# Holding 96 weight-sum transfers to their step with a small ScalarE copy, and laying them in three stages

## The chip, the cores and the metric

The kernel runs on one core of one Trainium2 chip. The metric is the device time of one execution in microseconds. The core has five engines that run their own instruction streams in order: PE (TensorE, matrix products), DVE (VectorE), ACT (ScalarE), POOL (GpSimd) and SP (SyncE, here only an issuer of transfers). Transfers run on 16 DMA engines; SP issues most of them, POOL those that this change is about.

## The reference, cut to what matters

The program is a two-layer decoder trunk over 1024 tokens of width 1024, in float32: a short gated convolution layer with a SwiGLU feed-forward block, then a latent-attention layer with a second SwiGLU block.

```python
def short_conv_mixer(h, w_in, conv_w, w_out):
    u = h @ w_in
    gate_b, gate_c, val = jnp.split(u, 3, axis=-1)
    z = gate_c * val
    conv = sum(conv_w[k] * zp[:, k:k + s] for k in range(CONV_WIDTH))   # zp: z, padded
    return (gate_b * conv) @ w_out

def swiglu_ffn(h, w13, w2):
    g, u = jnp.split(h @ w13, 2, axis=-1)
    return (jax.nn.silu(g) * u) @ w2

h = h + short_conv_mixer(rms_norm(h, conv_norm_g), conv_w_in, conv_w, conv_w_out)
h = h + swiglu_ffn(rms_norm(h, conv_ffn_norm_g), conv_ffn_w13, conv_ffn_w2)
k_nope, k_pe, v = shared_mla_kv(h, ...)
h = h + mla_mixer(rms_norm(h, mla_norm_g), ..., k_nope, k_pe, v, ...)
h = h + swiglu_ffn(rms_norm(h, mla_ffn_norm_g), mla_ffn_w13, mla_ffn_w2)
return rms_norm(h, final_norm_g)
```

## The kernel before

Every float32 product is made of three matmuls (`three`, lines 152 to 155) on a high and a low part of each operand. ACT makes the high part with a cast (line 112), and DVE or POOL subtracts it to get the low part (line 113). The large projections use a seven-product scheme for 2 x 2 blocks, which needs sums of blocks of the operands.

**Stages.** The program runs through: the conv input projection (class `Quad`, 12 quads of 7 products, tile `q`), the conv output projection (class `Plain`, tile `pl`), the up projection of the first feed-forward block (22 quads of 7 products, tile `q` again), its down projection (class `Down`, tile `dn`), the latents, the attention, and then `Plain`, up and `Down` once more for the second block. One product of a quad is 12 matmuls of 128x512.

**What sets the order.** Outside the attention the order is written by hand. `Steps` (lines 255 to 278) holds a list of PE work, one entry per product, and for each entry the functions to emit ahead of it (`before`) and behind it (`after`); all are emitted in that order, each to its own engine's stream. A step number is so a place in every stream, but nothing makes an engine wait for the step: an engine runs its stream as far ahead as its own waits let it. The attention is ordered by a planner; its order on PE, DVE and SP is the same in both kernels.

**The transfers that are changed.** `Down` needs, for four of its seven products, sums of blocks of the weight `w2`; these four sums (`mw_f` in DRAM, 6 groups each) are built for each feed-forward block with no compute engine at all, by transfers from DRAM to DRAM that POOL issues: a plain copy, or a copy that adds into its destination (`weight_sums`, lines 872 to 893; the issues are lines 889 and 887). Eight rounds over six groups make 48 transfers of 512 KB (256 KB for the last group) for each block, 96 in all. Line 887 waits for the transfers that it adds onto. `Down` loads the results on SP (line 613).

Before the change, lines 898 and 899 emit the first 48 at steps 4, 6, 8, ... of the conv input projection, and lines 908 and 909 the other 48 at steps 6, 9, 12, ... of the first up projection. POOL has in these stages one other task: in the conv input projection it forms two sums of weight columns for each quad (lines 377 and 380, two instructions of 128x512 for 12 quads).

**What stands around them.** SP's stream holds at the end of the conv input projection, in this order: loads of the stored conv result (`m<-md_conv`, line 548) and of the output weight (`wp`, line 503), eight loads of the residual stream (`h<-hd`, line 478, 512 KB each), the last two stores of the conv result (line 719), and the load of the last group of that result, which must wait for these stores. ACT splits that group (`mh<-m`, line 112) before PE can go on with `pl`. The up projections load a 512 KB tile of weights twice per quad (`wr`, line 361) into five buffers.

Of the kernel before, what the change touches and what calls it, by code (L numbers as in the profile page):

```python
# [9 lines left out]
F32 = mybir.dt.float32  # L10
# [6 lines left out]
P = 128  # L17
# [32 lines left out]
def trunk(ctx, tc, aps, out):  # L50
    nc = tc.nc
    A = aps
# [19 lines left out]
    small = ctx.enter_context(tc.tile_pool(name="small", bufs=2))  # L72
# [21 lines left out]
    def work(name, shape=None, dt=F32):  # L94
        return pslot(name, "t", 9, dt, shape or [P, S])
# [63 lines left out]
    ones = const.tile([P, P], F32, name="ones")  # L159
# [8 lines left out]
    for nm in ("conv_norm_g", "conv_w", "conv_ffn_norm_g", "kv_norm_g", "mla_norm_g", "kv_latent_norm_g",  # L168
               "mla_q_norm_g", "mla_ffn_norm_g", "final_norm_g"):
        a = A[nm]  # L170
        if len(a.shape) == 3:
            a = a.rearrange("a b c -> (a b c)")
        elif len(a.shape) == 2:
            a = a.rearrange("a b -> (a b)")
        n = a.shape[0] // P
# [71 lines left out]
    st = Stream()  # L247
    hd = dram.tile([KD, P, S], F32, name="hd")
    md = {"conv": dram.tile([KD, P, S], F32, name="md_conv")}
# [5 lines left out]
    class Steps:  # L255
# [13 lines left out]
        def run(self):  # L269
            end = max([len(self.pe)] + [n + 1 for n in (*self.pre, *self.post)])  # L270
            with tc.manual_schedule():
                for n in range(end):
                    for fn in self.pre.get(n, ()):
                        fn()
                    if n < len(self.pe):
                        self.pe[n]()
                    for fn in self.post.get(n, ()):
                        fn()
# [166 lines left out]
    def up(steps, quads, op):  # L445

        head, n0 = quads[:FILL], len(steps.pe)
        a, b = quads[:2]
        n = {}

        for x, i in [(a, 1), (b, 1), (a, 2), (b, 2), *((x, i) for x in head[2:] for i in (1, 2)),
                     *((x, i) for i in (5, 6, 7, 4, 3) for x in (a, b)),
                     *((x, i) for x in quads[2:] for i in ((5, 6, 7, 4, 3) if x in head else (1, 2, 5, 6, 7, 4, 3)))]:
            n[x, i] = x.add(steps, op, i)
        for x in head:
            steps.before(n[x, 1] - 9, x.load_a)
            steps.before(n[x, 1] - 2, x.pair)
        for x in quads:
            n5 = n[x, 5]
            if x in head:  # L460
                steps.before(n5 - 9, x.load_a, x.load_b)
            else:
                steps.before(n5 - 11, x.load_a)
                steps.before(n5 - 10, x.load_b)
                steps.before(n5 - 5, x.pair)
            e = 0 if x.eng is nc.vector else 1
            steps.before(n5 - 3 - e, x.sum3, x.sum1)
            steps.before(n5 - 2, lambda x=x: x.half(5))
            steps.before(n[x, 6] - 2, x.sum2, lambda x=x: x.half(6))
            steps.before(n[x, 7] - 2, lambda x=x: x.half(7))  # L470
            steps.before(n[x, 4] - 2, lambda x=x: x.half(4))
            steps.before(n[x, 3] - 2, x.sum4, lambda x=x: x.half(3))
        return n0
# [250 lines left out]
    steps = Steps()  # L724
# [99 lines left out]
    def ffn_quads(w13, m):  # L824
        wv = w13.rearrange("a k n -> (a k) n").rearrange("(k p) n -> p k n", p=P)

        first = {}

        def store(i, j, t):
            nc.sync.dma_start(m[i - 1, j], t)  # L830

        def one(j):

            last, j0, box = j >= KF // 2, j % (KF // 2), {}

            def product(c1, c2):
                nc.vector.tensor_tensor(c1, c1, c2, ALU.mult)
                store(2 if last else 1, j0, c1[:, :512])
                if last:
                    store(3, j0, c1[:, 512:])  # L840
                    box["b"] = [(c[:, :512], c[:, 512:]) for c in (first.pop(j0), c1)]
                else:
                    first[j] = c1

            def left(c1, c2):
                (b11, b12), (b21, b22) = box["b"]
                box["s"] = work("msum")
                box["t1"], box["t2"] = box["s"][:, :512], box["s"][:, 512:]
                sub(5, box["t1"], b12, b11)

            def right(c1, c2):
                (b11, b12), (b21, b22) = box["b"]
                sub(6, box["t2"], b22, box["t1"])

            def low(c1, c2):
                (b11, b12), (b21, b22) = box["b"]
                sub(7, b12, b22, b12)

            def corner(c1, c2):
                (b11, b12), (b21, b22) = box["b"]  # L860
                sub(4, b21, box["t2"], b21)

            def sub(i, o, x, y):
                nc.vector.tensor_tensor(o, x, y, ALU.subtract)
                store(i, j0, o)

            done = [product, left, right, low, corner] if last else [product]
            return Quad(wv, j * P, DFF + j * P, AF.Silu, done, nc.vector)

        return [one(j + f) for j in range(KF // 2) for f in (0, KF // 2)]  # L870

    def weight_sums(w, out):


        wv, half = w.rearrange("(k p) n -> p k n", p=P), KF // 2
        groups = [list(range(k, min(k + 2, half))) for k in range(0, half, 2)]

        def one(i, src, add, g):
            o = [out[j, g][:, :len(groups[g]) * 512].rearrange("p (k m) -> p k m", m=512) for j in range(4)]
            if isinstance(src, tuple):  # L880
                (a, b), k = src, groups[g][0]
                k += b * half
                src = wv[:, k:k + len(groups[g]), (1 - a) * 512:(2 - a) * 512]
            else:
                src = o[src]
            if add:
                nc.gpsimd.dma_start(o[i], src, accum_op=ALU.add)
            else:
                nc.gpsimd.dma_start(o[i], src)

        stages = ((0, (1, 0), False), (3, (0, 0), False), (0, (1, 1), True), (3, (1, 0), True),
                  (1, 0, False), (1, (0, 0), True), (2, 1, False), (2, (0, 1), True))
        return [[lambda st=st, g=g: one(*st, g) for g in range(len(groups))] for st in stages]

    flat = lambda w: w.rearrange("a k n -> (a k) n")
    kp = lambda w: w.rearrange("(k p) n -> p k n", p=P)
    pairs = lambda a, b: [list(range(k, min(k + 2, b))) for k in range(a, b, 2)]
    for j, fn in enumerate(x for stage in weight_sums(flat(A["conv_ffn_w2"]), md["f1w"]) for x in stage):
        steps.before(4 + 2 * j, fn)
    bd = Boundary("conv_ffn_norm_g")  # L900
    n0 = len(steps.pe)
    steps.before(n0, lambda: load_h(range(KD)))
# [2 lines left out]
    bd.first(steps, e[1] + 5, (e[1] + 7, e[1] + 9, e[1] + 11, e[1] + 13))  # L905
    bd.second(steps, e[3] + 1)
    n0 = up(steps, ffn_quads(A["conv_ffn_w13"], md["f1"]), bd.op)
    for j, fn in enumerate(x for stage in weight_sums(flat(A["mla_ffn_w2"]), md["f2w"]) for x in stage):
        steps.before(n0 + 6 + 3 * j, fn)


    rd = dram.tile([2, P, S], F32, name="rd")
# [133 lines left out]
    n0 = len(steps.pe)  # L1046
# [285 lines left out]
    steps = Steps()  # L1332
    bd = Boundary("mla_ffn_norm_g")
# [1 line left out]
    e = pl.ends  # L1335
    bd.first(steps, e[1] + 4, (e[1] + 5, e[1] + 6, e[1] + 6, e[1] + 7))
    bd.second(steps, e[3] + 1)
    up(steps, ffn_quads(A["mla_ffn_w13"], md["f2"]), bd.op)


    fnorm = Norm()
# [73 lines left out]
```

## Time and profile before

| what | value |
|---|---|
| median of 3 runs | 2308.64 us (2300.48 to 2309.67) |
| profiled execution, own time | 2309.89 us |
| its span, first to last instruction | 2308.1 us |
| mean granted clock of PE | 0.96 |
| conv input projection, first to last product | 28.1 to 291.5 us |
| conv output projection | 291.5 to 431 us |
| first up projection | 431 to 885 us |
| second up projection | 1604 to 2058 us |

The profile is one execution, with times counted from the start of its span. Rows of a group give busy time and mean duration, and the idle time of the engine just before with what ended it. A row of a list in order of time gives start, duration, engine, line, operation and tiles; a bracket gives the idle time before it and the releaser. A duration of a matmul overlaps the next one, so the pace of PE is read from start to start. "SPq" rows are transfers as SP issues them.

### The profile page before, as it was taken

Reading aid. Unit: us, or ns where it says so; the run is one execution under the profiler, and the core shown is the slowest. Engines: PE = TensorE matmul, PEld = TensorE weight load, DVE = VectorE, ACT = ScalarE, POOL = GpSimd, SP = SyncE. Lnnn points to the kernel's source line nnn. Section 1 sums busy time; section 2 is a strip of 40 time slices with the busy share of each in tenths; the row PEclk is TensorE's granted clock in tenths of the full one; section 3 lists DMA queues with packets and bytes.
Section 4 is the critical chain, followed back from the end, with each engine's and each line's share of the span. In section 5 each row is a group of like instructions: output and inputs, shape, how many; then the busy total and the mean of one; then the engine's idle time right before and its main releaser. Section 6 shows DMA issues by size and latency. Waiting matters only on the chain. (4 is left out here: it accounts for less than half of the span.)

```text
span 2308.1 us, 26314 instructions
## 1 busy us (share of the span) xinstructions
PE 2152.8 (93%) x9869; PEld 1770.5 (77%) x9869; DVE 1525.6 (66%) x2291; ACT 833.6 (36%) x1321; POOL 249.7 (11%) x286
## 2 busy tenths in 40 slices
PE   7889939889999999999987999998899999999997
PEld 5677827767888888788866888887777888888786
DVE  4787714587777776877335777636787777777554
ACT  6322313342333333345223555424433333333443
POOL 0232422100000000000114333210000000000000
PEclk9999978899999999999888999998899999999998
DMA  8366799914332328565212223423334233376542
GB/s 269 113 145 178 185 317 283 262 37 146 114 114 92 114 97 324 194 210 169 62 32 61 64 70 77 168 82 113 97 101 137 94 112 99 107 263 221 177 169 77
DMA packets 271341, 331.67 MB, mean 144 GB/s; under 512 B 17745, under 2 KB 178718, under 8 KB 270894
## 3 DMA queue, kind: packets, MB, share of 16 engines
q1 hardware_dynamic: 244144, 265.86, 35.1%
q0 software_dynamic: 26784, 64.04, 11.3%
q8 instruction: 77, 1.26, 0.2%
q14 instruction: 50, 0.41, 0.1%
q10 hardware_dynamic: 286, 0.11, 0.0%
HBM read 251.83 MB, written 119.01 MB: 161 GB/s over the span
## 5 line engine op out<-in xcount | busy, mean ns | idle before, releaser
L153 PE MATMUL q<-xh,w_hi 128*128 128x512 f32 x1568 | 623.6, 398 | 28.7 <-ACT w_hi L112 27.3
L155 PE MATMUL q<-xh,w_lo 128*128 128x512 f32 x1568 | 623.2, 397 | 11.2 <-DVE w_lo L113 11.0
L154 PE MATMUL q<-xl,w_hi 128*128 128x512 f32 x1568 | 619.2, 395 | 5.1 <-DVE xl L303 5.0
L113 DVE TENSOR_TENSOR w_lo<-wr,w_hi 128x1024 fp32r<-128x1024 f32 (+1 forms) x336 | 263.2, 783 | 212.9 <-ACT w_hi L112 212.7
L153 PEld LDWEIGHTS q<-xh,w_hi 128*128 128x128 f32 x1568 | 299.6, 191 | 100.6 <-ACT w_hi L112 38.8
L155 PEld LDWEIGHTS q<-xh,w_lo 128*128 128x128 f32 x1568 | 299.2, 191 | 91.1 <-DVE w_lo L113 28.8
L112 ACT CAST w_hi<-wr 128x1024 fp32r<-128x1024 f32 (+1 forms) x336 | 225.3, 686 | 353.9 <-DVE wr L386 197.9
L154 PEld LDWEIGHTS q<-xl,w_hi 128*128 128x128 f32 x1568 | 299.2, 191 | 68.9 <-DVE xl L303 6.7
L155 PE MATMUL dn<-mp_hi,wp_lo 128*128 128x512 f32 x616 | 242.2, 393 | 4.9 <-DVE wp_lo L113 3.2
L153 PE MATMUL dn<-mp_hi,wp_hi 128*128 128x512 f32 x616 | 242.1, 393 | 0.5 <-ACT wp_hi L112 0.5
L154 PE MATMUL dn<-mp_lo,wp_hi 128*128 128x512 f32 x616 | 240.7, 391 | 0.4 <-DVE mp_lo L113 0.4
L113 DVE TENSOR_TENSOR mp_lo<-m,mp_hi 128x1024 fp32r<-128x1024 f32 x84 | 95.3, 1135 | 128.5 <-ACT mp_hi L112 128.5
L112 ACT CAST mp_hi<-m 128x1024 fp32r<-128x1024 f32 x84 | 82.2, 979 | 215.0 <-PE dn L154 206.6
L155 PEld LDWEIGHTS dn<-mp_hi,wp_lo 128*128 128x128 f32 x616 | 115.9, 188 | 35.9 <-DVE wp_lo L113 12.0
L154 PEld LDWEIGHTS dn<-mp_lo,wp_hi 128*128 128x128 f32 x616 | 116.0, 188 | 25.1 <-DVE mp_lo L113 0.8
L153 PEld LDWEIGHTS dn<-mp_hi,wp_hi 128*128 128x128 f32 x616 | 116.0, 188 | 24.8 <-ACT wp_hi L112 1.9
L431 ACT ACTIVATE c<-c 128x512 f32<-128x512 f32 x44 | 27.8, 633 | 209.7 <-DVE c L409 209.7
L409 DVE TENSOR_TENSOR c<-q,c 128x512 f32<-128x512 f32 x112 | 76.8, 686 | 34.9 <-PE q L155 33.2
L113 DVE TENSOR_TENSOR wp_lo<-w,wp_hi 128x1024 fp32r<-128x1024 f32 x84 | 94.9, 1130 | 0.0
L153 PE MATMUL pl<-mh,wp_hi 128*128 128x512 f32 x128 | 52.5, 410 | 37.4 <-ACT mh L112 37.4
L112 ACT CAST wp_hi<-w 128x1024 fp32r<-128x1024 f32 x84 | 82.0, 976 | 0.0
L1014 POOL TENSOR_TENSOR wlat<-wlat,vec 128x1024 f32<-128x1024 f32 (+1 forms) x4 | 7.8, 1943 | 671.6 <-DMA wlat<-in_mla_w_dq_dram 671.6
(255 smaller groups left out, 3367.0 us busy)
## 6 DMA issues: line engine op xcount, KB each, us to landing
m<-md_f SPq DMA_DIRECT2D x70, 512.0 KB, 4.8
md_f<-c SPq DMA_DIRECT2D x110, 256.0 KB, 2.2
wr<-in_conv_ffn_w_dram SPq DMA_DIRECT2D x51, 512.0 KB, 4.3
wr<-in_mla_ffn_w_dram SPq DMA_DIRECT2D x51, 512.0 KB, 4.2
w<-mw_f SPq DMA_DIRECT2D x40, 512.0 KB, 4.9
wr<-in_conv_w_in_dram SPq DMA_DIRECT2D x32, 512.0 KB, 6.4
hd<-h SPq DMA_DIRECT2D x32, 512.0 KB, 5.0
h<-hd SPq DMA_DIRECT2D x32, 512.0 KB, 9.1
```

The lines of the kernel that those rows point to most:

```text
L112: nc.scalar.copy(out=hi, in_=src)
L113: (eng or nc.vector).tensor_tensor(lo, src, hi.bitcast(F32), ALU.subtract)
L153: nc.tensor.matmul(ps, lhsT=wh, rhs=xh, start=st, stop=False)
L154: nc.tensor.matmul(ps, lhsT=wh, rhs=xl, start=False, stop=False)
L155: nc.tensor.matmul(ps, lhsT=wl, rhs=xh, start=False, stop=en)
L409: add = lambda o, a: nc.vector.tensor_tensor(o, b, a, ALU.add)
L431: nc.scalar.activation(self.C1[:, 512:], self.C1[:, 512:], self.first)
L1014: self.eng.tensor_tensor(v, v, g.broadcast_to([P, KD, self.m]), ALU.mult)
```

## The change

The 96 transfers become one list, still in the same sequence: the 48 of the first block, then the 48 of the second. Each is now emitted by `paced`: ACT copies a column of ones into a tile of one element per partition, POOL copies that tile into another, and then POOL issues the transfer. POOL's copy waits for ACT's, and POOL runs its stream in order, so that the transfer cannot be issued before ACT has come to this place in its own stream.

The list is laid out in three places: 21 transfers at steps 16, 20, ..., 96 (the conv input projection has the steps 0 to 83, the conv output projection 84 to 115); 35 at steps 14, 18, ..., 150 of the first up projection (which has 154); and the other 40 in the second up projection, from its step 2 on, at intervals of three and four steps.

```diff
-        return [[lambda st=st, g=g: one(*st, g) for g in range(len(groups))] for st in stages]
+        return [lambda st=st, g=g: one(*st, g) for st in stages for g in range(len(groups))]
+
+    def paced(steps, n, fn):
+
+        def run():
+            a, b = [small.tile([P, 1], F32, name=nm, bufs=16) for nm in ("pace", "paced")]
+            nc.scalar.copy(out=a, in_=ones[:, 0:1])
+            nc.gpsimd.tensor_copy(b, a)
+            fn()
+        steps.before(n, run)
...
-    for j, fn in enumerate(x for stage in weight_sums(flat(A["conv_ffn_w2"]), md["f1w"]) for x in stage):
-        steps.before(4 + 2 * j, fn)
+    sums = [x for w, out in (("conv_ffn_w2", "f1w"), ("mla_ffn_w2", "f2w")) for x in weight_sums(flat(A[w]), md[out])]
+    for n in range(16, 100, 4):
+        paced(steps, n, sums.pop(0))
...
-    for j, fn in enumerate(x for stage in weight_sums(flat(A["mla_ffn_w2"]), md["f2w"]) for x in stage):
-        steps.before(n0 + 6 + 3 * j, fn)
+    for n in range(n0 + 14, n0 + 154, 4):
+        paced(steps, n, sums.pop(0))
...
-    up(steps, ffn_quads(A["mla_ffn_w13"], md["f2"]), bd.op)
+    n0 = up(steps, ffn_quads(A["mla_ffn_w13"], md["f2"]), bd.op)
+    for j, fn in enumerate(sums):
+        paced(steps, n0 + 2 + 7 * j // 2, fn)
```

The streams of PE, DVE and SP hold the same instructions in the same order as before. ACT's gains 96 copies, POOL's gains 96 copies, and the 96 transfers change their place in POOL's. The first place is POOL at the start of the program; L377 and L380 are its sums for the quads of the conv input projection, and `mw_f` is the DRAM tensor of weight sums. Before:

```order
L889 DMA mw_f_93<-in_conv_ffn_w_dram 256x1x512 x3
L377 ISA
L377 TENSOR_TENSOR wr<-wr 128x512
L380 TENSOR_TENSOR wr<-wr 128x512
L889 DMA mw_f_93<-in_conv_ffn_w_dram 256x1x512
L377 TENSOR_TENSOR wr<-wr 128x512
```

And now, where line 900 is POOL's copy in `paced`:

```order
L377 ISA
L377 TENSOR_TENSOR wr<-wr 128x512
L380 TENSOR_TENSOR wr<-wr 128x512
L377 TENSOR_TENSOR wr<-wr 128x512
L380 TENSOR_TENSOR wr<-wr 128x512
L900 COPY paced<-pace 128x1
L889 DMA mw_f_93<-in_conv_ffn_w_dram 256x1x512
```

Three transfers stood ahead of everything else; now the first stands behind the sums of two quads and a copy that waits for ACT. The second place is POOL at the end of the conv input projection, with the last quad's sums. Before:

```order
L377 TENSOR_TENSOR wr<-wr 128x512
L380 TENSOR_TENSOR wr<-wr 128x512
L889 DMA mw_f_93<-mw_f_93 16x8192 x5
L889 DMA mw_f_93<-mw_f_93 128x512
L887 DMA mw_f_93<-in_conv_ffn_w_dram 256x1x512 x5
L887 DMA mw_f_93<-in_conv_ffn_w_dram 128x512
L889 DMA mw_f_95<-in_mla_ffn_w_dram 256x1x512 x5
L889 DMA mw_f_95<-in_mla_ffn_w_dram 128x512
```

And now:

```order
L377 TENSOR_TENSOR wr<-wr 128x512
L380 TENSOR_TENSOR wr<-wr 128x512
L900 COPY paced<-pace 128x1
L887 DMA mw_f_93<-in_conv_ffn_w_dram 256x1x512
L900 COPY paced<-pace 128x1
L887 DMA mw_f_93<-in_conv_ffn_w_dram 256x1x512
L900 COPY paced<-pace 128x1
L887 DMA mw_f_93<-in_conv_ffn_w_dram 128x512
```

Behind the last sums stood sixty transfers in one run; now each has a copy ahead of it that waits for ACT. The third place is ACT at the start of the second up projection, where `xh` is the high part of an operand, `w_hi` that of a weight, L199 a root for the norm and L416 the silu. Before:

```order
L199 ACTIVATE r<-var 128x4
L112 CAST w_hi<-wr 128x1024
L416 ACT_TABLE_LOAD
L416 ACTIVATE c_12352<-c_12352 128x512
L416 ACTIVATE c_12369<-c_12369 128x512
L112 CAST w_hi<-wr 128x1024
L412 COPY c_12463<-q 128x512
L302 CAST xh<-xraw 128x1024
```

And now:

```order
L199 ACTIVATE r<-var 128x4
L112 CAST w_hi<-wr 128x1024
L899 COPY pace<-ones 128x1
L416 ACT_TABLE_LOAD
L416 ACTIVATE c_12536<-c_12536 128x512
L416 ACTIVATE c_12553<-c_12553 128x512
L112 CAST w_hi<-wr 128x1024
L412 COPY c_12652<-q 128x512
L302 CAST xh<-xraw 128x1024
L899 COPY pace<-ones 128x1
```

ACT's own work keeps its order; a copy of one element per partition stands between.

## The prediction

> **What bounds the kernel now.** I read the slices of the page first, then the windows where they sag, then the timelines of the engines there.
>
> ```profile
> PE 2152.8 (93%) x9869; PEld 1770.5 (77%) x9869; DVE 1525.6 (66%) x2291; ACT 833.6 (36%) x1321; POOL 249.7 (11%) x286
> ...
> PE   7889939889999999999987999998899999999997
> ...
> DMA  8366799914332328565212223423334233376542
> ```
>
> PE is the bound, with a hole in the sixth slice (288 to 346 us). DMA is full there and for three slices more. The next view, the instructions on the weight sums' tensor, says what filled it.
>
> ```profile
> L887 POOL DMA_DIRECT2D mw_f<-in_conv_ffn_w_dram x24: 832/1134/2501, 117.4 to 285.1; - x24
> L889 POOL DMA_DIRECT2D mw_f<-mw_f x24: 488/508/1321, 196.8 to 412.5; - x24
> L887 POOL DMA_DIRECT2D mw_f<-in_mla_ffn_w_dram x24: 824/1030/1157, 321.8 to 419.9; - x24
> L889 POOL DMA_DIRECT2D mw_f<-in_conv_ffn_w_dram x12: 536/774/982, 1.9 to 116.8; - x12
> L889 POOL DMA_DIRECT2D mw_f<-in_mla_ffn_w_dram x12: 536/651/1177, 285.6 to 319.3; - x12
> DMA to landing us min/median/max: 2.9/10.8/30.6
> ```
>
> The columns behind a count are ns of issue (least, median, most), then the first and last start. Nothing held these transfers: all 48 sums of the second block, needed after 2058 us, were issued between 285.6 and 420, exactly where PE has its hole. Now PE, ACT, DVE and SP in order of time.
>
> ```profile
> 308.59 0.39 PE L155 MATMUL pl<-mh,wp_lo 128*128 128x512 f32 x1
> 346.37 0.79 PE L153 MATMUL pl<-mh,wp_hi 128*128 128x512 f32 x1 [37.39 <-ACT mh L112]
> ...
> 353.34 0.40 PE L155 MATMUL pl<-mh,wp_lo 128*128 128x512 f32 x1
> ```
> ```profile
> 345.27 1.04 ACT L112 CAST mh<-m 128x1024 fp32r<-128x1024 f32 x1 [40.27 <-DMA m<-md_conv]
> ```
> ```profile
> 295.30 2.35 DVE L718 TENSOR_TENSOR conv<-conv,c 128x1024 f32<-128x1024 f32 x2
> ```
> ```profile
> 285.50 18.74 SPq L478 DMA_DIRECT2D h<-hd  x8
> 306.72 0.32 SPq L719 DMA_DIRECT2D md_conv<-conv  x1
> 309.36 0.38 SPq L503 DMA_DIRECT2D wp<-in_conv_w_out_dram  x1
> 311.83 0.32 SPq L719 DMA_DIRECT2D md_conv<-conv  x1
> 335.04 0.37 SPq L548 DMA_DIRECT2D m<-md_conv  x1
> ```
>
> PE waits 37.4 us for a load. DVE had the last conv results ready at 297.65, SP could store the last only at 311.83, the store took 23.2 us (to 335.04) and the load 10.2 (to 345.27). A view of windows shows that nothing but transfers moved meanwhile.
>
> ```profile
> 308.70:345.00 36.30, 0.28 (x2) 0.00 (x0) 0.00 (x0) 0.00 (x0) 12.26 (x14) 0.55 1.05 338
> ...
> 433.00:460.00 27.00, 21.04 (x84) 16.69 (x84) 8.81 (x17) 8.13 (x12) 0.00 (x0) 0.75 0.85 253
> 1604.00:1632.00 28.00, 23.80 (x96) 19.30 (x95) 20.27 (x32) 12.57 (x18) 0.00 (x0) 0.76 0.59 188
> 530.00:885.00 355.00, 354.29 (x1550) 289.46 (x1550) 267.15 (x388) 112.97 (x185) 0.00 (x0) 1.00 0.38 120
> 1700.00:2058.00 358.00, 357.28 (x1563) 291.81 (x1562) 269.28 (x390) 113.09 (x186) 0.00 (x0) 1.00 0.38 121
> ```
>
> Columns: window, length, busy time and count of PE, PEld, DVE, ACT, POOL, granted clock, DMA share, GB/s. From 308.7 to 345 the engines stand, DMA is at 1.05 of its 16 engines with 338 GB/s: that is the rate of a full DMA. In the two up projections, where 75 transfers go now, DMA is at 0.38 and PE has no idle time worth naming (354.29 of 355).
>
> A second wait follows at the start of the first up projection.
>
> ```profile
> 438.50 1.04 ACT L112 CAST w_hi<-wr 128x1024 fp32r<-128x1024 f32 x1 [10.23 <-DMA wr<-in_conv_ffn_w_dram]
> ```
> ```profile
> 439.60 0.79 PE L153 MATMUL q<-xh,w_hi 128*128 128x512 f32 x1 [5.92 <-ACT w_hi L112]
> 441.45 0.63 PE L153 MATMUL q<-xh,w_hi 128*128 128x512 f32 x1
> 441.88 0.63 PE L154 MATMUL q<-xl,w_hi 128*128 128x512 f32 x1
> ...
> 444.87 0.63 PE L155 MATMUL q<-xh,w_lo 128*128 128x512 f32 x1
> ```
>
> PE loses 5.9 us to a weight that lands late, and then starts matmuls 0.43 us apart (441.45 to 441.88) instead of 0.23 (355 us for 1550).
>
> **The first stall, after the change.** The change leaves SP's stream as it is, so the eight `h` loads still stand ahead of the stores. What goes is the traffic beside them. From 285.5 SP has to move eight loads, one `wp` and two stores, 11 x 0.524 MB = 5.8 MB. At the full 338 GB/s that is 17 us, and about one paced transfer of 0.524 MB falls into that time (steps four products apart, 4 x 12 matmuls x 0.229 = 11 us), 1.6 us more: the last store is landed near 304, and not before 297.65 + 2.9 (the least landing of the rows above) = 300.6. The load adds between 4 and 10.2 us (the wait above; a weight load in a half empty DMA takes 4.2, row below), cast and first matmul 1.1 (345.27 to 346.37). That is 306 to 316 against 308.8, when PE is through with the groups it has: a wait of 0 to 7. I take 4, towards the slow end since `wp` and `h` loads still crowd there: **33.4 us** gained. Bounds: all 37.4, or only half (18.7) if the loads of SP alone keep the DMA full.
>
> After the wait PE runs slowly from 346.37 to 353.34, 7.0 us for 14 matmuls (346.37 to 353.34) that need 3.2 at 0.229, 3.8 us lost. A wait of 4 us may bring that back or not; I take half, **1.9** (0 to 3.8).
>
> The Trainium skill ("TensorE: Matmul & The Clock Gate", Part 1: The HAM clock gate) has the clock back after about 3.4 us of steady work. This trace took twice as long, 7 us. By the page the slow phase would cost about 1.7 us and the term would be 0.85 in place of 1.9.
>
> **The second stall.** At 433 nothing of the weight sums will be in flight but one paced transfer per 11 us, so the weight lands in time: **5.9 us**, and of the 12 matmuls from 439.60 to 444.87, which take 5.7 us with the last one's 0.43 and need 2.7 at 0.229, **3 us**. The same place of the second block (1604 to 1632), without any such traffic, still shows a clock of 0.76, since the norm's small matmuls lie there; so I don't take more. Bounds: 0, if another wait takes the place (the second block has one of its own there, on DVE), to 9.
>
> **The conv input projection and the start.** Three transfers at 1.9 us no longer run beside the first loads of `x`; 18 more leave the stage or are spread. PE's stalls there end on ACT and DVE, which follow POOL's sums:
>
> ```profile
> L380 POOL TENSOR_TENSOR wr<-wr 128x512 f32<-128x512 f32 x12 | 20.4, 1700 | 0.9
> L377 POOL TENSOR_TENSOR wr<-wr 128x512 f32<-128x512 f32 x12 | 16.7, 1388 | 203.0 <-DMA wr<-in_conv_w_in_dram 120.8 <-DVE w_lo L113 68.2 <-ACT conv L709 14.1
> ```
>
> SP's loads there wait for buffers that the products free, so that I expect little: **1 us**, from -4 to 6. The loss would come from POOL: a sum now stands behind a copy that waits for ACT and an issue of about 1.1 us (median of line 887 above). A sum is emitted two steps, or 5.5 us, ahead of its cast; the two sums (1.4 and 1.7) and the issue are 4.2. That fits, with 1.3 us to spare.
>
> **The copies.** 96 on ACT and 96 on POOL. The trace has no ACT copy of one column; the nearest row is a root of four columns, and for POOL a fill of one column.
>
> ```profile
> L199 ACT ACTIVATE r<-var x11: 205/206/209, 18.8 to 2298.5; 128x4 f32<-128x4 f32 x8, 128x8 f32<-128x8 f32 x3
> ```
> ```profile
> 0.24 0.10 POOL L1404 MEMSET const-float32-0.0<- 128x1 f32 x1 [0.24 <-issue]
> ```
>
> 96 x 0.21 = 20 us of ACT, spread over stages where ACT is busy a third of the time (112.97 of 355): hidden by that idle time. They show only where PE waits for ACT, in the first 20 steps of the second up projection, where five or six copies stand: 1.2 us at most. Without the cover it would be 20. Behind a waiting POOL copy in the up projections only other weight sums are queued; in the conv stages POOL's sums, reckoned above.
>
> **The transfers in the up projections.** 35 and 40 of them now run beside the weight loads.
>
> ```profile
> wr<-in_conv_ffn_w_dram SPq DMA_DIRECT2D x36, 512.0 KB, 4.2
> ```
> ```profile
> 711.66 1.19 SPq L361 DMA_DIRECT2D wr<-in_conv_ffn_w_dram  x2
> ```
> ```profile
> 728.23 1.22 DVE L113 TENSOR_TENSOR w_lo<-wr,w_hi 128x1024 fp32r<-128x1024 f32 x1 [0.26 <-ACT w_hi L112]
> ```
>
> A load is issued at 711.66 and lands in 4.2 us; the cast ahead of 728.23 uses it at about 727. Slack 11 us, so that a load must take over 15 us before PE feels it. One transfer of 0.524 MB at 338 GB/s takes 1.6 us of the DMA, every 11 us: the share rises from 0.38 to about 0.53. I expect no stall in the steady part and, with the copies, **-3 us** for the crowded starts of the two stages (0 to -12).
>
> **Sum.** 33.4 + 1.9 + 5.9 + 3 + 1 - 3 = 42 us off the profiled execution's 2309.9, so 2268. That execution lies 1.3 us above the median of the three runs, so against the median I say **2267 us**.
>
> **The rivals.** *The load stays late.* SP's own `h`, `wp` and `m` loads keep the DMA full between 285 and 320, and half of the first stall stays (18.7 us less 4, and the slow phase): 42 - 16 = 26 gained, **2283**. For it: the store waits behind 4 MB of `h` in the same queue, and that is not changed. Against it: the twelve transfers of line 889 from 285.6 to 319.3 alone, ten of 0.524 MB and two of half that, are 5.8 MB, as much as SP moved itself.
>
> *Late weights in the up projections*, the case on the slower side. If a paced transfer makes the weight load beside it land as late as transfers did in the full DMA, every second quad's first load (22 in the two stages) comes late. Landing at 20 us, between the median 10.8 and the most 30.6 above, is 4.7 us past the 15.5 (4.2 + 11) that is free; 22 x 4.7 = 103 us lost, 42 gained, **2370**. It decides from a mean of about 17.5 us on (2 us x 22 = 42). Against it: DMA at half load. A mild form, 1.5 us on each, eats 33 and leaves about 2300.
>
> The Trainium skill ("DMA: Bandwidth & Descriptors", Queues, rings and completion order) lets each DMA engine serve its queues by turns, packet by packet. By it a load beside one transfer takes at most twice its time, 8.4 us instead of 4.2, inside the slack, and this rival has no chance; the 23.2 us of the store agree with a halved queue. I leave it some, since no row shows the two together at half load.
>
> *The hold doesn't hold.* ACT's copy reads a constant, so it is held by nothing but ACT's order; if ACT ran far ahead, transfers would bunch as before and nothing would change, 2309. Against it: ACT also empties PE's banks (lines 412 and 419), once or twice in every seven products, and cannot pass a product that PE hasn't made.
>
> *More goes*: both stalls vanish, and the conv stage gains its 6: 37.4 + 3.8 + 9 + 6 = 56, **2253**.
>
> **How the numbers follow.** Forecast 58%, load stays late 20%, more goes 8%, mild lateness 6%, strong lateness 5%, no hold 3%. The range 2248 to 2294 takes in the forecast, the first rival and most of the last, with the unknown terms (conv stage -4 to 6, up projections 0 to -12). What a measurement can tell from no change is about 0.5%, 11.5 us, so faster means under 2297: the first three cases, 86%. The mild case and no hold are no change, 9%; 5% slower.
>
> **What would show it.** Right: no `mw_f` issue ahead of 75 us, 40 of them after 1604; PE's wait for `mh` below 10 us and none for `w_hi` at 433; DMA near 0.5 in the up projections with PE still full. Wrong: a wait for `mh` near 18 us with DMA at 1 and few `mw_f` beside it; waits of PE on `w_hi` after 530 or 1700; POOL's sums starting later than their loads, followed by waits on `w_lo` in the conv input projection.

## Result, and the profile after

The changed kernel takes 2249.41 us (median of four runs, 2246.52 to 2250.66), the kernel before beside it 2308.84 us (four runs, 2300.48 to 2309.67): a ratio of 0.9749, 95% interval 0.9724 to 0.9773, or 59 us less. Timed a second time, against another set of runs, it took 2253.67 us against 2304.01: 0.9784 (0.9769 to 0.9800), 50 us less. The forecast was 2267 with a range from 2248 to 2294: the direction and the main mechanism held, but the gain was forecast too small, and the measured time lies close to the lower end of the range.

The page of the profile after, with a span of 2244.8 us:

```profile
PE 2134.0 (95%) x9869; PEld 1757.0 (78%) x9869; DVE 1524.2 (68%) x2291; ACT 841.4 (37%) x1417; POOL 308.9 (14%) x382
...
PE   7989989899999999999969999999899999999997
...
DMA  7234684156555576564022123524377565685551
```

The hole of PE in the sixth slice is gone. DMA is no longer full for three slices (the 9s of before, 288 to 462 us); in the two up projections it is now at 0.58 and 0.65 (windows shown under dense_up below). The instructions on the weight sums' tensor say that the transfers lie where they were put:

```profile
L887 POOL DMA_DIRECT2D mw_f<-in_conv_ffn_w_dram x24: 818/1026/1104, 233.5 to 730.3; - x24
L889 POOL DMA_DIRECT2D mw_f<-in_conv_ffn_w_dram x12: 536/654/694, 94.1 to 225.0; - x12
L887 POOL DMA_DIRECT2D mw_f<-in_mla_ffn_w_dram x24: 817/1022/1087, 1618.7 to 1952.3; - x24
DMA to landing us min/median/max: 3.0/5.1/10.4
```

The first starts at 94.1 us instead of 1.9, the last at 1952.3 instead of 419.9. The median time to landing on this tensor is 5.1 us in place of 10.8; the view counts SP's loads of the finished sums in it too. At the place of the first stall, in order of time: PE, ACT, SP.

```profile
308.43 0.80 PE L153 MATMUL pl<-mh,wp_hi 128*128 128x512 f32 x1 [5.97 <-ACT mh L112]
```
```profile
307.33 1.04 ACT L112 CAST mh<-m 128x1024 fp32r<-128x1024 f32 x1 [20.32 <-DMA m<-md_conv]
```
```profile
279.91 5.36 SPq L478 DMA_DIRECT2D h<-hd  x8
290.30 0.32 SPq L719 DMA_DIRECT2D md_conv<-conv  x1
290.72 0.38 SPq L503 DMA_DIRECT2D wp<-in_conv_w_out_dram  x1
291.43 0.32 SPq L719 DMA_DIRECT2D md_conv<-conv  x1
302.80 0.37 SPq L548 DMA_DIRECT2D m<-md_conv  x1
```

PE waits 5.97 us in place of 37.39. SP is through with the eight `h` loads in 5.36 us (18.74 before), the last store takes 11.4 us (291.43 to 302.80; 23.2 before) and the load 4.5 (302.80 to 307.33; 10.2 before).

To see where the time went, I cut each profile where PE changes from one tile to the next (`q` to `pl` to `q` to `dn` and so on), and did the same for a second profile of each kernel, taken later. Lengths in us:

| stage | before | before, second | after | after, second |
|---|---|---|---|---|
| start to first `q` | 28.1 | 28.0 | 26.7 | 26.9 |
| conv input projection | 263.4 | 259.6 | 259.2 | 261.0 |
| conv output projection | 139.2 | 142.0 | 99.0 | 98.6 |
| first up projection | 454.7 | 452.7 | 444.0 | 444.0 |
| first down projection, latents, attention | 680.3 | 677.8 | 675.2 | 680.2 |
| attention's output projection | 38.3 | 37.1 | 37.1 | 35.5 |
| second up projection | 453.3 | 453.1 | 452.8 | 454.2 |
| second down projection and end | 250.6 | 250.7 | 250.7 | 250.8 |

Only two stages differ by more than they do from profile to profile of one kernel: the conv output projection and the first up projection, together 50.9 us in the first pair and 52.1 in the second. The rest of the change in span is -12.4 us in the first pair and +2.4 in the second. I read the 59 us of the first comparison and the 50 of the second as some 51 or 52 us of effect each, and several us that come and go.

### The profile page after: what moved, and what is told of

It is laid out like the page before. It is cut to its first block, busy times and chain, and to the rows that moved or that the text cites. A ratio compares the mean times of both kernels' runs of the same rounds, so it can differ in the third digit from the quotient of the medians.

```text
span 2244.8 us, 26510 instructions
## 1 busy us (share of the span) xinstructions
PE 2134.0 (95%) x9869; PEld 1757.0 (78%) x9869; DVE 1524.2 (68%) x2291; ACT 841.4 (37%) x1417; POOL 308.9 (14%) x382
## 5 line engine op out<-in xcount | busy, mean ns | idle before, releaser
L900 POOL COPY paced<-pace 128x1 f32<-128x1 f32 x96 | 68.0, 708 | 1014.8 <-ACT pace L899 1014.8
L648 DVE TENSOR_TENSOR h<-h,dn 128x512 f32<-128x512 f32 x112 | 71.4, 679 | 4.4 <-PE dn L155 4.4
```

Source lines behind the costliest of these rows:

```text
L648: nc.vector.tensor_tensor(hv, hv, banks[q], ALU.add if sign > 0 else ALU.subtract)
L900: nc.gpsimd.tensor_copy(b, a)
```

## The experiments

**Undoing the hold, keeping the layout (layout_only).** The transfers stay in the three places, but the two copies ahead of each go:

```diff
     def run():
-        a, b = [small.tile([P, 1], F32, name=nm, bufs=16) for nm in ("pace", "paced")]
-        nc.scalar.copy(out=a, in_=ones[:, 0:1])
-        nc.gpsimd.tensor_copy(b, a)
         fn()
```

> The three places of the change without the copies, so that nothing holds the transfers. Theory (the hold does it): POOL passes its last column sum of the conv input projection near 265 us and lets 41 transfers loose at once, 19 MB, where 60 went before; SP's store and load still share a full DMA from 285 on, PE's wait for the split of the last conv group stays at 25 to 37 us. The other 40 go in one run when POOL is done with the attention's transfers, near 1480, and crowd the start of the second output projection: 0 to 20 us lost there. Time 2285 to 2320. Rival (where they stand is enough): the wait falls below 10 us and the time to 2265 or less.

Measured: 2323.53 us, ratio to before 1.0095 (1.0072 to 1.0118): 1% slower than the kernel before, and just above the range expected. Its instructions on the tensor of the sums, and the start of POOL's list in order of time:

```profile
L887 POOL DMA_DIRECT2D mw_f<-in_mla_ffn_w_dram x24: 827/1030/1252, 374.1 to 464.6; - x24
L889 POOL DMA_DIRECT2D mw_f<-in_mla_ffn_w_dram x12: 536/700/1181, 1.9 to 372.4; - x12
DMA to landing us min/median/max: 3.1/14.3/30.3
```
```profile
1.94 2.65 POOL L889 DMA_DIRECT2D mw_f<-in_mla_ffn_w_dram  x4
...
264.66 1.29 POOL L377 TENSOR_TENSOR wr<-wr 128x512 f32<-128x512 f32 x1 [14.01 <-DVE w_lo L113]
266.03 1.62 POOL L380 TENSOR_TENSOR wr<-wr 128x512 f32<-128x512 f32 x1
267.60 9.17 POOL L887 DMA_DIRECT2D mw_f<-in_conv_ffn_w_dram  x9
```

No transfer is left for the second up projection: all 96 are issued before 465 us. Four that the code emits for the second up projection are the first transfers of the sums, at 1.94 us, ahead of the whole program, and right after the last column sum of the conv stage nine go out at once. So the description of the kernel above is not right for these 40: their step is not a place in POOL's stream, and without a tie to a compute engine they went ahead of work that the code emits far earlier. Why they were put there is not shown. PE's wait for `mh` became 46.6 us (25 to 37 expected), and the first up projection grew to 472.7, with waits of 9.6, 4.8 and 3.4 us for `w_hi` at its start. The expected heap of transfers near 1480 us did not come. Since the third place of the layout was never reached, the run does not test the layout without the hold; it shows that without the two copies there is no such layout. The copies do two things: they keep POOL from running ahead, and they fix the place of the transfer at all.

**Keeping the hold, undoing the layout (hold_only).** All 96 are held, but at the steps of before: 4, 6, 8, ... in the conv input projection, and 6, 9, 12, ... in the first up projection.

```diff
-    for n in range(16, 100, 4):
-        paced(steps, n, sums.pop(0))
+    for j in range(48):
+        paced(steps, 4 + 2 * j, sums.pop(0))
...
-    for n in range(n0 + 14, n0 + 154, 4):
-        paced(steps, n, sums.pop(0))
+    for j in range(48):
+        paced(steps, n0 + 6 + 3 * j, sums.pop(0))
```

> The copies and the hold, at the steps of the kernel before (every second step of the conv input projection from 4 on, every third of the first up projection from 6 on), nothing in the second up projection. Theory (the hold does it): one transfer per 5.4 us in the conv stage and per 8 us in the up stage, none in a heap; PE's wait for the last conv group is 5 to 12 us, the rest as after the change; 2245 to 2262. Rival (the spread over three stages matters): the denser transfers bring late weights in the conv input projection or the first up projection, more than 2275.

Measured: 2258.35 us, 0.9808 (0.9782 to 0.9834), 45 us below before. PE's wait for `mh` is 8.1 us, the first up projection 445.6; what it lacks against the change lies mostly in the conv input projection, 266.9 us instead of 259 to 261 in its one profile. So the hold alone brings most of the gain, and the layout perhaps 6 to 8 us; the interval of hold_only lies apart from that of the change in the first comparison (0.9724 to 0.9773) and overlaps that of the second (0.9769 to 0.9800). DMA is busier in that stage, 0.69 between 110 and 285 us where the change has 0.48, but this is not the cause: second_only, the next kernel, has 0.72 there and takes 260.5 us. The same window of hold_only, then of second_only (columns as in the prediction):

```profile
110.00:285.00 175.00, 165.64 (x701) 133.62 (x700) 137.59 (x166) 52.45 (x107) 66.61 (x81) 0.97 0.69 166
```
```profile
110.00:285.00 175.00, 167.49 (x725) 135.48 (x724) 136.56 (x172) 52.39 (x80) 62.76 (x60) 0.99 0.72 177
```

Held transfers at every second step put twice as many waiting copies between POOL's column sums; whether this costs the 6 us stays open.

**Only the second block's transfers (second_only).** The first block's 48 go unheld, as before; the second block's 48 are held in the second up projection, one every three steps.

```diff
-    for n in range(16, 100, 4):
-        paced(steps, n, sums.pop(0))
+    for j in range(48):
+        steps.before(4 + 2 * j, sums.pop(0))
...
-    for n in range(n0 + 14, n0 + 154, 4):
-        paced(steps, n, sums.pop(0))
...
-        paced(steps, n0 + 2 + 7 * j // 2, fn)
+        paced(steps, n0 + 2 + 3 * j, fn)
```

> The 48 sums of the first block unheld at the steps of the kernel before, the 48 of the second block held in the second up projection. Theory: the dose counts. From 268 on 12 transfers instead of 60 run beside SP's loads, 5.8 MB beside SP's 5.8 MB and what it had in flight: the store lands near 311, PE's wait is 10 to 16 us, the weight at the start of the first up projection is in time; 2255 to 2275. It also shows the conv input projection and the start with the old, unheld sums: if their 5.6 us of gain came from the hold, that stage is as long as before the change (263 us and a start at 28.1); if not, as after it (259).

Measured: 2264.18 us, 0.9835 (0.9813 to 0.9857), 39 us below before. PE and SP at the place of the first stall:

```profile
322.88 0.80 PE L153 MATMUL pl<-mh,wp_hi 128*128 128x512 f32 x1 [17.09 <-ACT mh L112]
```
```profile
282.55 18.53 SPq L478 DMA_DIRECT2D h<-hd  x8
303.46 0.32 SPq L719 DMA_DIRECT2D md_conv<-conv  x1
306.16 0.38 SPq L503 DMA_DIRECT2D wp<-in_conv_w_out_dram  x1
307.22 0.32 SPq L719 DMA_DIRECT2D md_conv<-conv  x1
317.38 0.37 SPq L548 DMA_DIRECT2D m<-md_conv  x1
```

The `h` loads are as slow as before (18.53 us) beside the first block's transfers, the last of which is issued at 282.9; the last store behind them is fast again (307.22 to 317.38 is 10.2 us, 23.2 before). The wait of 17.09 us is a little above the 10 to 16 expected. Holding the second block's transfers so takes 20 us off the wait, and holding the first block's as well another 11. The conv output projection without its wait for `mh` is 110.1 - 17.1 = 93.0 us, the same as in the change (99.0 - 6.0); in the two profiles of before it is 101.8 and 105.0. There is more in that stage than the wait, and the second block's transfers are what takes it. The conv input projection took 260.5 us with the first block's transfers unheld, as much as in the change.

**The `h` loads behind the stores (late_h, and again as late_h_again).** The change, with the eight loads of `h` three steps later, so that the stores of the conv result stand ahead of them in SP's stream.

```diff
-    steps.before(n0, lambda: load_h(range(KD)))
+    steps.before(n0 + 3, lambda: load_h(range(KD)))
```

> The change, with the eight loads of the residual stream moved three steps back on SP, behind the last two stores of the conv result and the load that waits for them. Theory (what is left of PE's wait, 6.0 us, is SP's own loads ahead of the store): the store lands 3 to 5 us after its issue, the wait falls to 0 to 2 us, and nothing else moves, since the first eviction that needs the residual stream has 8 banks to wait in; 2238 to 2246. Rival (the wait is the latency of store and load one after the other): it stays at 4 to 6 us and the time at 2249.

> The change with the eight loads of h three steps later in SP's stream, behind the conv stage's stores. Theory (what is left of the wait for mh, 6.0 us, is SP's own h loads ahead of the stores, and goes with them): 4 to 6 us below the change in the same call, 2242 to 2246, wait for mh 0. Rival (the wait goes but comes back, since h lands later and the stores now share the DMA with other loads, or chance is as large): within 2 us of the change.

Measured: 2246.97 us, 0.9760 (0.9741 to 0.9780), and again 2246.81 us, 0.9752 (0.9738 to 0.9765). The change, run beside the second of these, took 2253.67, with a wait of 6.21 us:

> The change, unchanged, beside the next two kernels on the same chip. 2246 to 2251 us, ratio to before 0.973 to 0.978; wait for mh 4 to 8 us again.

The change is itself a little above what was expected. Beside the same runs of before, the two intervals of the ratio do not meet (0.9738 to 0.9765 against 0.9769 to 0.9800): late_h_again is faster, by 6.9 us. Against the change's first timing (0.9749) neither run of the version differs. What the profiles show is 4.5 to 4.9 us in the conv output projection, 94.1 in both instead of 99.0 and 98.6; in late_h_again 3.3 of them are missing again in the first up projection (447.3 instead of 444.0; 444.0 in late_h), so that the gain of the whole is not known as closely as that of the stage. PE and SP of late_h:

```profile
306.75 0.51 PE L153 MATMUL pl<-mh,wp_hi 128*128 128x512 f32 x1 [1.33 <-ACT mh L112]
```
```profile
293.26 0.34 SPq L719 DMA_DIRECT2D md_conv<-conv  x1
293.70 0.37 SPq L503 DMA_DIRECT2D wp<-in_conv_w_out_dram  x1
294.39 0.55 SPq L719 DMA_DIRECT2D md_conv<-conv  x1
301.12 0.37 SPq L548 DMA_DIRECT2D m<-md_conv  x1
301.58 4.44 SPq L478 DMA_DIRECT2D h<-hd  x8
```

The last store is landed after 6.7 us (294.39 to 301.12) instead of 11.4, and the wait is 1.33 us (0.89 in late_h_again), not quite none as expected. What was left of the first stall was for the most part the 4 MB of `h` loads standing ahead of the stores, as the prediction's first rival had it, but for 5 us and not for 19.

**The kernel before, profiled again (before_again).**

> The kernel before, unchanged, profiled a second time. Question: are the 680.3 us from the first down projection to the end of the attention, and the 263.4 us of the conv input projection, a property of this kernel or of that one execution? If chance (my reading, since three of the four variants so far have 674 to 676 there, also the one that unholds everything): 674 to 677 and 258 to 264, and the wait for mh again 35 to 40 us. If they belong to the kernel before: 679 to 682 and 262 to 265 again, and the change gains some 5 us after its last transfer of the first block.

Its two changed stages repeat (142.0 and 452.7, wait for `mh` 36.95). The stage of the first down projection, latents and attention took 677.8, and 680.3 belongs to neither kernel: over all thirteen profiles of this study this stage is at 674 to 678 us in ten, and at 680 to 681 in three: the first of before, the second of the change, and dense_up below. The 5.1 us by which it seems to gain in the first pair come and go.

**Nothing in the conv stage at all (ups_late_h).** With the late `h` loads, the first block's 48 are held in the first up projection and the second block's 48 in the second, one every three steps.

```diff
-    for n in range(16, 100, 4):
-        paced(steps, n, sums.pop(0))
...
-    for n in range(n0 + 14, n0 + 154, 4):
+    for n in range(n0 + 2, n0 + 146, 3):
         paced(steps, n, sums.pop(0))
...
-        paced(steps, n0 + 2 + 7 * j // 2, fn)
+        paced(steps, n0 + 2 + 3 * j, fn)
```

> No weight sums in the conv stage at all: 48 of the first block held in the first up projection, one every three steps, 48 of the second in the second, one every three steps; h loads three steps later as in the kernel beside it. Theory (transfers in the up projections are free as long as a weight load has 11 us of slack; without them the conv input projection has DMA and POOL to itself, 19 copies and issues less): conv input projection 254 to 259, both up projections within 1 us of 444 and 453, 2240 to 2245. Rival (denser transfers make weights late, or the stage's time is set by DVE and ACT anyway): up projections 446 to 460, 2246 to 2265; if only the conv stage doesn't move, level with the kernel beside it, 2243 to 2247.

Measured: 2247.25 us, 0.9753 (0.9733 to 0.9773), with runs from 2238.51 to 2251.97. Its profile (the fastest of these runs) has 256.4 us for the conv input projection, 93.0 for the output projection, 445.6 and 453.1 for the up projections. By the median it is level with late_h_again, and above the 2240 to 2245 expected; that it is better is not shown.

**The price of transfers beside weight loads (dense_up).** The second block's 48 go into the first up projection too, one transfer every second step there, none in the second.

```diff
-    for n in range(n0 + 14, n0 + 154, 4):
+    for n in range(n0 + 2, n0 + 152, 2):
         paced(steps, n, sums.pop(0))
```

> The 21 transfers of the conv stage stay; the other 75 all go into the first up projection, one every second step (one per 5.5 us in place of one per 11), none into the second. This prices the case that transfers make weight loads late. Theory (a weight load has 11 us of slack, and a DMA at 0.53 plus 40 more transfers of 0.524 MB, near 0.65 to 0.7, lands it well inside): first up projection 444 to 447, second 452 to 454, whole kernel 2246 to 2255, no wait of PE for w_hi beyond that of the change. Rival (late weights): each transfer beside a load eats the slack, waits of PE on w_hi in most of the 22 quads, first up projection above 455, whole kernel above 2262.

Measured: 2252.84 us, 0.9782 (0.9769 to 0.9796), level with the change. The windows of the two up projections, first of the change, then of dense_up (columns as in the prediction), and dense_up's weight loads, the last column their median time from issue to landing:

```profile
485.00:829.00 344.00, 343.30 (x1501) 280.30 (x1501) 257.57 (x373) 112.31 (x210) 46.74 (x62) 1.00 0.58 163
1640.00:1994.00 354.00, 353.36 (x1546) 288.56 (x1545) 266.37 (x386) 115.24 (x217) 52.36 (x66) 1.00 0.65 168
```
```profile
485.00:829.00 344.00, 343.14 (x1498) 279.65 (x1498) 257.67 (x373) 115.16 (x241) 88.06 (x124) 1.00 0.79 204
1640.00:1994.00 354.00, 353.31 (x1546) 288.58 (x1545) 266.48 (x387) 112.27 (x185) 0.00 (x0) 1.00 0.37 117
```
```profile
wr<-in_conv_ffn_w_dram SPq DMA_DIRECT2D x51, 512.0 KB, 7.0
wr<-in_mla_ffn_w_dram SPq DMA_DIRECT2D x51, 512.0 KB, 4.2
```

With DMA at 0.79 PE is as full as with 0.58 or 0.37: 343.14 of 344 us against 343.30. The first up projection took 444.7 us instead of 444.0. The weight loads landed in a median of 7.0 us in place of the second block's 4.2, and in 13.3 at most where the trace has a landing (23 of 51): inside the 15 that are free. The share of DMA rose further than the 0.65 to 0.7 expected.

**The price of the copies (copies_x4, copies_x16).** Four, then sixteen copies of ACT ahead of each transfer.

```diff
-            nc.scalar.copy(out=a, in_=ones[:, 0:1])
+            for _ in range(4):
+                nc.scalar.copy(out=a, in_=ones[:, 0:1])
```

> The change with four copies on ScalarE ahead of each transfer in place of one: 288 more, at 0.186 us each 54 us of ScalarE's time, in bursts of 0.75 us. Theory (hidden by ScalarE's idle time): 2247 to 2256, every stage within 2 us of the change's two profiles. Rival (ScalarE is on the path where copies stand, so that one copy costs its time): up to 54 us more, 2300.

> The same with sixteen copies: 1440 more, 268 us of ScalarE's time, in bursts of 3.0 us. Theory (hidden as long as a burst is shorter than the slack of a weight's cast): the steady parts of the up projections unmoved, a few us at their starts and in the conv input projection, where products follow casts at a short distance; 2250 to 2275. Rival (on the path): a good part of 268 us, above 2350. If it lies between, the difference by stage over the number of bursts there (21, 35, 40) is the price of one burst and 3.0 less that is the cover.

Measured: 2254.02 us for four, 0.9799 (0.9784 to 0.9814), which can't be told from the change's 0.9784 (the intervals overlap, and the stages below agree); 2328.13 for sixteen, 1.0111 (1.0095 to 1.0128), the whole gain and more. ACT, of copies_x4 and then of copies_x16, at one pace:

```profile
603.47 0.86 ACT L900 COPY pace<-ones 128x1 f32<-128x1 f32 x4
```
```profile
606.41 3.53 ACT L900 COPY pace<-ones 128x1 f32<-128x1 f32 x16
```

| stage | bursts | the change | four (0.86 us) | sixteen (3.53 us) | per burst of sixteen |
|---|---|---|---|---|---|
| conv input projection | 21 | 259.2, 261.0 | 260.4 | 270.5 | 0.5 |
| first up projection | 35 | 444.0, 444.0 | 444.2 | 468.4 | 0.7 |
| second up projection | 40 | 452.8, 454.2 | 454.0 | 491.5 | 0.95 |

The last column is the stage with sixteen less the mean of the change, by the count. A burst of 0.86 us is covered as far as the profiles can tell. Of 3.53 us some 2.6 to 3.0 are covered on average, and the rest is paid. A burst is 3.34 us longer than the change's one copy (3.53 less 0.19), 321 us more of ACT for 96 of them, and 74 to 79 us of that show in the time (2328.13 less 2253.67 or 2249.41): between the two theories, and above the 2275 at which the first one ended.

## Why the prediction was right, and where it was off

**The first stall**: right. Forecast was a wait of 0 to 7 us, 4 taken, 33.4 gained; measured 5.97 and 6.21, that is 31.4 and 30.7 gained. That the heap of transfers makes the wait, and that SP's `h` loads keep a rest of it, is what layout_only, second_only and late_h show. That the size came out so well is in part luck. The clock readings look alike (last store landed at 302.80, forecast 304; matmul at 308.43, forecast 306 to 316), but the stage began 5.6 us earlier. Counted from the first `h` load, the store landed after 22.9 us (279.91 to 302.80) where the forecast had 18.5 (285.5 to 304): 4.4 late. SP issued it only at 291.43, right behind DVE's result (289.05 and 2.35 us), and it then took 11.4 us, while the forecast of 304 went by the bytes at the full rate. The load made up for it with 4.5 us, at the fast end of 4 to 10, where a wait of 4 us stands for some 7.7 (304 + 7.7 + 1.1 = 308.8 + 4).

**The slow phase after it**: 1.9 forecast. In the first pair PE's excess over 0.227 us a matmul there falls from 3.8 to 3.1 us, in the second it goes from 2.3 to 2.5. Nothing was gained for certain: behind a wait of 6 us the granted clock falls to a half as it does behind one of 37 us (0.51 before and 0.50 after, third column from the end). Even late_h's wait of 1.33 us is followed by matmuls 0.43 us apart, 2.8 us of excess.

```profile
346.37:353.40 7.03, 6.56 (x15) 4.80 (x16) 2.34 (x2) 0.90 (x1) 1.45 (x2) 0.51 1.09 260
```
```profile
308.43:313.70 5.27, 4.81 (x11) 3.46 (x12) 2.34 (x2) 0.89 (x1) 0.00 (x0) 0.50 1.05 397
```

The Trainium skill ("TensorE: Matmul & The Clock Gate", Part 1: The HAM clock gate) has the full clock back after about 3.4 us of work. The four slow phases last 7.0 and 3.6 us before and 5.3 and 4.0 after (from the first matmul to the last that starts 0.43 after the one ahead of it), so the skill's figure is near the shortest of them, and the 7 us of the prediction was the longest.

**The second stall**: right, within the two profiles. 5.9 + 3 = 8.9 were forecast; the stage gained 10.7 and 8.7. No wait for `w_hi` stands at that place any longer. In the second profile of before this wait was 4.1 us instead of 5.9, so that some 2 us of the term differ from one execution to the next.

**The up projections**: -3 forecast for crowded starts, 0 measured. The first up projection is at 444.0 with 35 transfers and 444.7 with 75; the second at 452.8 and 454.2 with 40 and 452.8 with none (dense_up). With it falls the rival of late weights, which held 11 of 100: it needed a mean landing of 17.5 us, and the median landings were 5.4 in the change and 7.0 in dense_up. The slack of 11 us was the right number to look at. (The prediction adds it to the 4.2 of a load as 15.5; it is 15.2, which changes nothing. And its page shows DMA full for two slices behind the sixth, not three.)

The Trainium skill's turns by packet ("DMA: Bandwidth & Descriptors", Queues, rings and completion order) gave the prediction an estimate of at most 8.4 us for a load beside one transfer. Both medians lie below it, but it is no limit for single loads here: of those with a landing in the trace, 6 of 49 in the change took 8.5 to 10.2 us, and 7 of 23 in dense_up took more than 8.4, up to 13.3. Whether these met more than one transfer is not shown.

**The copies**: right, hidden; copies_x4 shows no cost with four times ACT's copies.

**The stall that was missed.** The terms for the conv output projection and the first up projection came to 41.2 us (33.4 + 1.9 + 8.9 - 3); measured are 50.9 and 52.1. Of the difference, 4.8 us in the first pair and 2.8 in the second lie in the first up projection, for the most part the 3 us for crowded starts that were not paid. The rest, 4.9 and 8.1 us, lies in the conv output projection, and above all at a third stall that the prediction did not have, since it read only the two places where the waits were longest. These are PE, DVE, ACT and SP of before in order of time:

```profile
388.02 0.39 PE L155 MATMUL pl<-mh,wp_lo 128*128 128x512 f32 x1
391.00 3.57 PE L214 MATMUL sp<-ones,nsq 128*128 128x1 f32 x16 [2.59 <-DVE nsq L667]
394.44 0.77 PE L153 MATMUL pl<-mh,wp_hi 128*128 128x512 f32 x1
395.01 0.63 PE L154 MATMUL pl<-ml,wp_hi 128*128 128x512 f32 x1
...
399.89 1.13 PE L230 MATMUL rp<-dg,ones 128*128 128x512 f32 x2 [0.93 <-DVE dg L221]
400.45 0.79 PE L153 MATMUL pl<-mh,wp_hi 128*128 128x512 f32 x1
```
```profile
387.38 1.23 DVE L113 TENSOR_TENSOR wp_lo<-wp,wp_hi 128x1024 fp32r<-128x1024 f32 x1 [4.77 <-ACT wp_hi L112]
```
```profile
386.30 1.05 ACT L112 CAST wp_hi<-wp 128x1024 fp32r<-128x1024 f32 x1 [3.61 <-DMA wp<-in_conv_w_out_dram]
```
```profile
357.35 1.36 SPq L503 DMA_DIRECT2D wp<-in_conv_w_out_dram  x1
```

PE waits 2.59 us for the norm's squares on DVE. DVE had stood 4.77 us behind the low part of a weight `wp` that it takes first, ACT waited for the high part, and ACT for the load of `wp`, issued at 357.35 and landed some 29 us later, while the second block's transfers went (the `wp` loads of the change take 4 to 9 us there): a weight that PE itself does not need yet holds up the norm behind it. Then PE's small sums run slowly (3.44 us from 391.00 to 394.44), as do the matmuls behind them. In the change the same piece reads:

```profile
349.62 1.84 PE L214 MATMUL sp<-ones,nsq 128*128 128x1 f32 x16
351.32 0.48 PE L153 MATMUL pl<-mh,wp_hi 128*128 128x512 f32 x1
...
354.17 1.03 PE L230 MATMUL rp<-dg,ones 128*128 128x512 f32 x2
354.63 0.80 PE L153 MATMUL pl<-mh,wp_hi 128*128 128x512 f32 x1
```

From the sums to the matmul behind the second wait it is 5.0 us (349.62 to 354.63), without a wait; before, from the end of the last matmul ahead at 388.25 (388.02 and 0.23) to 400.45, it is 12.2. That is 7.2 us; in the second pair the same piece goes from 15.1 us (382.79 to 397.91) to 5.0, 10.1 us. The 40.2 us by which the stage became shorter in the first pair are so made up of 31.4 for the first wait, 0.7 for the slow phase, 7.2 here and 0.9 that I can't place; the 43.4 of the second pair of 30.7, -0.2, 10.1 and 2.8. The two terms forecast for this stage (33.4 and 1.9) were somewhat too large, and the missing term more than made up for that. second_only, which holds the second block's transfers alone, has the stage without its wait at 93.0 us, as the change has; so the second block's transfers make this stall, while the way through the late `wp` is read from these rows and was not tried by itself.

**The conv input projection and the start**: +1 forecast (-4 to 6); 5.6 in the first pair, -0.3 in the second, within the bounds. second_only has 260.5 us there without any hold in that stage, so nothing shows that the change's 259.2 is the hold's doing. ups_late_h, with no transfer there, has 256.4: 3 to 5 us less than the change, in one profile.

**The rivals.** "The load stays late" is half true in kind (SP's own `h` loads do hold the stores) but is worth 5 us, not 19. "The hold doesn't hold" falls with the profile of the change, where the transfers go from 94.1 to 1952.3 us; layout_only shows what happens without the copies. "More goes", 2253, is nearest to the measured time, but for another reason than it gave: the first stall did not vanish, and the conv stage did not gain for certain; a third stall went.

## What to carry to other kernels

A transfer that waits for no compute engine can start far from the step where the code names it (at 1.9 us in layout_only instead of in the second up projection): hold it with a tiny copy on an engine that is paced by the bound, and check in the trace that the issues are where the code puts them. When a full DMA is taken away, look for all short waits in its time, also those whose releaser is a compute engine: in an in-order stream a late weight shows up at whatever stands behind its cast. And before transfers are thinned out, look at the slack of the loads that run beside them: with 11 us of slack for a load of 4 us, a DMA at 0.79 cost nothing here.

## What was not expected of the hardware

POOL's copy of one column is recorded with a median of 0.616 us (0.177 to 1.267) in the change, six times the fill of one column, which took 0.10. In copies_x16, where sixteen of ACT's copies stand ahead of it, the same copy takes 0.185 us:

```profile
L900 POOL COPY paced<-pace x96: 177/616/1267, 93.0 to 1951.2; 128x1 f32<-128x1 f32 x96
```
```profile
L901 POOL COPY paced<-pace x96: 175/185/1002, 95.8 to 2033.7; 128x1 f32<-128x1 f32 x96
```

What the longer record contains stays open; in the up projections only transfers stand behind it on POOL. ACT's copy, of which the prediction had only a root of four columns at 0.206 us, takes 0.186. PE's slow phase after a wait of 37 us lasted 7.0 and 3.6 us in two profiles of the same kernel, so that a term for it can't be set closer than by some 3 us from one profile.
